# A float32 decoder trunk on one core: the stationary operands' buffers are laid 64 and 32 bytes further apart

## The chip, the core and the metric

The kernel runs on one core of a Trainium2 chip. The metric is the time of one execution on the device, in microseconds (us); of several runs the median is taken. An engine of the core is named as in the profile: PE is TensorE's matmul, PEld TensorE's weight load, DVE VectorE, ACT ScalarE, POOL GpSimd, SP SyncE.

## What is computed

One layer of a "macaron" decoder on 256 tokens of width 2048, in float32. The reference, cut to what matters:

```python
def swiglu(h, w_gate, w_up, w_down):
    return (jax.nn.silu(h @ w_gate) * (h @ w_up)) @ w_down

def hybrid_mixer(h, w_in, conv_w, pool_w, pool_scale, w_out):
    z = h @ w_in                                  # 2048 x 5120
    ...
    return jnp.concatenate([y_attn, y_conv, y_pool], axis=-1) @ w_out

for l in range(DEPTH):                            # DEPTH = 1
    x = x + FFN_RESIDUAL * swiglu(rmsnorm(x, ffn1_norm[l]), ffn1_w_gate[l], ffn1_w_up[l], ffn1_w_down[l])
    x = x + hybrid_mixer(rmsnorm(x, mix_norm[l]), w_in[l], conv_w[l], pool_w[l], pool_scale[l], w_out[l])
    x = x + FFN_RESIDUAL * swiglu(rmsnorm(x, ffn2_norm[l]), ffn2_w_gate[l], ffn2_w_up[l], ffn2_w_down[l])
return rmsnorm(x, final_norm)
```

The feed-forward width is 5632. Between the mixer's two products stand dilated attention, a short convolution and a pooling over windows, all small beside the products.

## The kernel before

Every large product `x @ W` is one job of `gemm` (L138): it makes a block of 256 tokens by 512 columns in PSUM, over row blocks `k` of 128. Both operands are split into a high and a low part, and three matmuls per `k` and token tile `t` are summed (L161 to L163): high activations by high weights, low by high, high by low. In each of them the stationary operand (loaded into the array ahead of the matmul, one weight load per matmul) is a 128x128 piece of the activations, and the moving operand is a 128x512 piece of the weights:

```python
nc.tensor.matmul(acc_of[t][:, t, :], lhsT=hi[:, ts], rhs=wh[:, i, :], start=first, stop=False)
nc.tensor.matmul(acc_of[t][:, t, :], lhsT=lo[:, ts], rhs=wh[:, i, :], start=False, stop=False)
nc.tensor.matmul(acc_of[t][:, t, :], lhsT=hi[:, ts], rhs=wl[:, i, :], start=False, stop=last)
```

The weights come in by SP's queue as `wt` (L171), four row blocks at a time; ACT rounds them into `wh` (L177) and DVE makes `wl`, the rest (L178).

The jobs are named by their sums. `ag` and `au` (gate and up product, 11 column blocks each, in groups of six and five) and `az` (the mixer's input product, 10 column blocks) take the activations `xh`, `xl`: the residual stream, transposed and split by `gained` (L242), four column blocks of `[P, 4, S]`, each 4096 bytes on a partition. `ad` (the down product) takes `hh`, `hl`, the transposed hidden blocks (L255 on, in `ffn`), and `ao` (the mixer's output product) takes `yh`, `yl`; these come from `act_tile` (L44), twelve buffers of 4096 bytes that the mixer's other tiles (`zq`, `qt` and so on) and the last norm's gains `gf` use too. A feed-forward runs 12 jobs `ag`, `au`, then 4 jobs `ad` over 24 row blocks, then 10 jobs and 4 jobs `ad` over 20 row blocks. With 6 matmuls per row block these are 1152, 576, 960 and 480 matmuls; `az` has 960, `ao` 384. Over the kernel `ag`, `au` and `az` have 5184 matmuls, `ad` and `ao` 2496, together 7680.

The order of the instructions is made by a scheduler ahead of the run; the buffers of one tag lie one behind the other in SBUF in the order in which the tags first appear.

Of the kernel before, what the change touches and what calls it, by code (L numbers as in the profile page):

```python
# [9 lines left out]
F32R = mybir.dt.float32r  # L10
# [4 lines left out]
AX = mybir.AxisListType  # L15

P = 128
NB = 512          # columns of one product (one PSUM bank)
CH = 4            # 128-row blocks of a weight per load
EPS = 1e-6  # L20
NEG = -1e30

# [2 lines left out]
def hybrid_trunk(ctx, tc, x, ffn1_norm, ffn1_w_gate, ffn1_w_up, ffn1_w_down, mix_norm, w_in,  # L25
                 conv_w, pool_w, pool_scale, w_out, ffn2_norm, ffn2_w_gate, ffn2_w_up,
                 ffn2_w_down, final_norm, out):
    """Every large product x @ W runs as three one-pass float32r products. An operand a is split
    exactly into ah (a rounded to 12 significant bits) and al = a - ah (at most 12 bits), and
    ah bh + ah bl + al bh is summed in float32."""  # L30
    nc = tc.nc
    B, S, D = x.shape
    T = S // P                      # token tiles
    DN = D // NB                    # column blocks of the model dimension
    FF = ffn1_w_gate.shape[2]
    FB = FF // NB
    KD = D // P
# [3 lines left out]
    pool = ctx.enter_context(tc.tile_pool(name="sb", bufs=1))  # L41
    psum = ctx.enter_context(tc.tile_pool(name="ps", bufs=2, space=bass.MemoryType.PSUM))

    def act_tile(shape, dt, name):  # L44
        return pool.tile(shape, dt, name=name, tag="act", bufs=12)

    def work(shape, name, dt=F32):
        return pool.tile(shape, dt, name=name, tag="wk", bufs=5)
# [1 line left out]
    def tp_tile(name):  # L50
        return psum.tile([P, 2 * NB], F32, name=name, tag="tp", bufs=2)

# [1 line left out]
    xr = [pool.tile([P, T, NB], F32, name=f"x{n}") for n in range(DN)]  # L54
    xv = x[0].rearrange("(t p) d -> p t d", p=P)

    def load_x(n):
        nc.sync.dma_start(out=xr[n], in_=xv[:, :, n * NB:(n + 1) * NB])

    # Per-channel parameters: rows of 128 channels, transposed onto partitions.  # L60
    small, col = [], {}
    for l in range(DEPTH):
        for key, src in (("ffn1", ffn1_norm[l:l + 1]), ("mix", mix_norm[l:l + 1]),
# [26 lines left out]
    make_identity(nc, ident)  # L90
    mhalf = pool.tile([P, T], F32, name="mhalf")
    nc.gpsimd.memset(mhalf, -0.5)
    # While the first loads are under way: ScalarE's tables, TensorE's clock.
    early = pool.tile([P, T], F32, name="early")
    nc.scalar.activation(out=early, in_=mhalf, func=AF.Silu)
    spin = tp_tile("spin")
# [1 line left out]
        nc.tensor.transpose(spin[:, :P], ident, ident)  # L98
    place_params(first_params)

    # C[q, k]: in how many of the patterns key k is for query q; columns 0..127: queries 0..127
    # and keys 0..127; the rest: queries 128..255 and keys 0..255.
    NK = 3 * P
    cnt = pool.tile([P, NK], F32, name="cnt")
    bia = pool.tile([P, NK], F32, name="bia")
# [26 lines left out]
                                    op0=ALU.min)  # L132
        nc.vector.reciprocal(out=rcnt, in_=rcnt)

# [1 line left out]
    high = [None]                   # the last of the weights' roundings  # L136
    later = []                      # work to be put between the products of a job

    def gemm(lhs, w, n0, ks, name, cuts=None, before=None, by_tile=None):
        """lhs: k -> (high, low) [P, S] of block k; w: [K, N] in DRAM, row blocks ks, columns  # L140
        n0.. -> [P tokens, T, NB] in PSUM. cuts: row blocks per load; before(k): called ahead of
        block k's load; by_tile(t, acc): token tile t is multiplied whole before the next one,
        and this is called when it is done."""
        def bank_pair():
            return psum.tile([P, T, NB], F32, name=name, tag="acc", bufs=2)

        acc = bank_pair()
        acc_of = [acc] * T
        if by_tile:
            acc_of = [acc] + [bank_pair() for _ in range(T - 1)]  # L150
        nk = len(ks)
        c0 = 0
        held = []

        def products(t, c0, kk, wh, wl):
            ts = slice(t * P, (t + 1) * P)
            for i, k in enumerate(kk):
                hi, lo = lhs(k)
                first, last = c0 + i == 0, c0 + i == nk - 1
                acc = acc_of[t]  # L160
# [4 lines that stand above are left out]
        cuts = cuts or [CH] * (nk // CH)  # L165
        for ci, m in enumerate(cuts):
            kk = ks[c0:c0 + m]
            if before:
                before(kk[0])
            wt = pool.tile([P, CH, NB], F32, name="wt", tag="wt", bufs=4)  # L170
            nc.sync.dma_start(  # L171
                out=wt[:, :m],
                in_=w[kk[0] * P:(kk[-1] + 1) * P, n0:n0 + NB].rearrange("(k p) n -> p k n", p=P))
            wh = pool.tile([P, CH, NB], F32R, name="wh", tag="wh", bufs=3)
            wl = pool.tile([P, CH, NB], F32R, name="wl", tag="wl", bufs=3)
            with nullcontext() if before else tc.high_priority():
                high[0] = nc.scalar.activation(out=wh[:, :m], in_=wt[:, :m], func=AF.Copy)  # L177
                nc.vector.tensor_sub(out=wl[:, :m], in0=wt[:, :m], in1=wh[:, :m].bitcast(F32))  # L178
            if by_tile and ci >= len(cuts) - 3:
                held.append((c0, kk, wh, wl))  # L180
            else:
                for i, k in enumerate(kk):
                    for t in range(T):
                        products(t, c0 + i, [k], wh[:, i:i + 1], wl[:, i:i + 1])
            c0 += m
            step()
        if by_tile:
            for t in range(T):
                for h in held:
                    products(t, *h)  # L190
                by_tile(t, acc_of[t])
        return acc
# [6 lines left out]
        while later:  # L199
            step()  # L200

# [1 line left out]
    def new_stats():  # L203
        return pool.tile([P, T, DN], F32, name="ss", tag="ss", bufs=2)

# [14 lines left out]
        return rs  # L220

    def transposed(src):
        """[P tokens, T, 4 P] -> PSUM [P, 4, S]"""
        tp = tp_tile("tp").rearrange("p (k s) -> p k s", k=4)
        for i in range(4):
            for t in range(T):
                nc.tensor.transpose(tp[:, i, t * P:(t + 1) * P], src[:, t, i * P:(i + 1) * P], ident)
        return tp
# [1 line left out]
    Q = 32  # L230

    def turned(src, dst):
        """The same by VectorE, SBUF [P, 4, S]: 32 x 32 blocks, moved between the quadrants."""
        sv = src.rearrange("p t (k j c) -> p k t j c", j=P // Q, c=Q)
        dv = dst.rearrange("p k (t a r) -> p k t a r", t=T, a=P // Q)
        for a in range(P // Q):
            for j in range(P // Q):
                nc.vector.transpose(out=dv[j * Q:(j + 1) * Q, :, :, a, :],  # L238
                                    in_=sv[a * Q:(a + 1) * Q, :, :, j, :])
        return dst  # L240

    def gained(n, c0, at_once=False):  # L242
        """Column block n of the residual, times the norm's gain, transposed and split."""
        tp = transposed(xr[n]) if at_once else turned(xr[n], work([P, 4, S], "xt"))
        hi = pool.tile([P, 4, S], F32R, name="xh", tag="xh", bufs=4)
        lo = pool.tile([P, 4, S], F32R, name="xl", tag="xl", bufs=4)
        for i in range(4):
            g = prm[:, c0 + 4 * n + i:c0 + 4 * n + i + 1]
            nc.scalar.activation(out=hi[:, i, :], in_=tp[:, i, :], func=AF.Copy, scale=g)  # L249
# [19 lines left out]
            nc.vector.scalar_tensor_tensor(out=xr[n][:, t, :], in0=acc[:, t, :], scalar=factor,  # L269
                                           in1=xr[n][:, t, :], op0=ALU.mult, op1=ALU.add)  # L270

# [1 line left out]
    def ffn(xt, rs, wg, wu, wd, after, cuts=None, before=None, last_tile=None):  # L273
        """x += 1/2 SwiGLU; after(n) when column block n of x is done; rs() gives the rows' norm
        factors. cuts, before: for the first product; last_tile(t): in place of after() for the
        last column block."""
        ht = {}

        def hidden(j, **first):
# [27 lines left out]
        for j0 in range(0, FB, 6):  # L307
# [3 lines left out]
            ks = range(4 * js[0], 4 * js[-1] + 4)  # L311
# [10 lines left out]
                if done:  # L322
                    after(n)

# [1 line left out]
    def mixer(l, xt, rs_of, after):  # L326
        HD = 64
        rs = rs_of()
# [21 lines left out]
            later.append(turn)  # L350

        def attend(half, i, zs):
            """Two heads, in three steps."""
            parts = (slice(0, P), slice(P, NK))
            st = {}

# [29 lines left out]
            def turn():  # L386
                p = st["p"]
                pt_ps = tp_tile("ptp").rearrange("p (j c) -> p j c", j=2)
                for j in range(2):
                    for a in range(3):  # L390
                        cs = slice(a * P, (a + 1) * P)
                        nc.tensor.transpose(pt_ps[:, j, cs], p[:, j, cs], ident)
                # keys 0..127 by queries 0..255, then keys 128..255 by queries 128..255
                st["pt"] = work([P, 2, NK], "pt")
                nc.scalar.activation(out=st["pt"], in_=pt_ps[:, :, :NK], func=AF.Copy)

# [17 lines left out]
        def attention_half(half):  # L414
# [2 lines left out]
            z_transposed(zs, "k", half)  # L417
            zs["v"] = z_block("v", half)
            pairs = [attend(half, i, zs) for i in range(4)]
            for r in range(6):          # step r - i of pair i  # L420
                def together(r=r):
                    for i in (2, 1, 0, 3):
                        if 0 <= r - i < 3:
                            pairs[i][r - i]()
                later.append(together)
# [76 lines left out]
            residual(acc, n, 1.0)  # L502
            after(n)

# [1 line left out]
    def phase(key, l, body):  # L506
        """Statistics and transposed blocks of the residual for the next sub-layer are made as
        its column blocks are finished."""
        ss, nxt = new_stats(), {}

        def after(n):
# [7 lines left out]
        rs = rstd_of(ss)  # L519
        return nxt, lambda: rs  # L520

    # The first sub-layer's blocks of x are loaded and transposed between its first weights.
    ss0, xt, r0 = new_stats(), {}, []

    def first_block(k):
# [10 lines left out]
            later.extend([lambda: place_params(more), masks, pool_consts])  # L536
        return r0[0]

    # The last norm, by token tiles.
    gf = {}  # L540
    sf = [pool.tile([P, 1, DN], F32, name=f"sf{t}") for t in range(T)]
    xg = {}
# [76 lines left out]
```

## Time and profile before

| | |
|---|---|
| median of 2 runs | 1807.97 us (1807.80 to 1808.13) |
| span of the profiled execution, first to last instruction | 1806.0 us |
| what lies around the span, by the median | 1.97 us |
| PE busy in that span | 1792.2 us (99%) |
| DVE, ACT busy | 1144.4 us (63%), 748.4 us (41%) |
| moved by DMA | 342.32 MB, mean 190 GB/s |

The page names for the profiled execution its span alone; it has no time of its own beside it. A matmul's duration runs from its start to its modelled end and overlaps the next matmul's; how fast PE works is therefore read from the distance between starts, or from a stage's length by its count of matmuls.

### The profile page before, as it was taken

The numbers are of one execution on the slowest core, as the hardware profiler recorded it, in microseconds if no ns is written. First come the engines' busy times: TensorE is split into PE (matmuls) and PEld (weight loads), VectorE is DVE, ScalarE is ACT, GpSimd is POOL, SyncE is SP. The second block draws the span as 40 slices with busy tenths as digits, with TensorE's granted clock in tenths as the row PEclk, the third lists the DMA queues.
The fourth block names the chain that finished last, engine by engine and source line by source line (L and its number), as shares of the span: only waits on it lengthen the run. The fifth ranks groups of instructions, "written<-read, shape, count | busy, mean of one in ns | idle before, by whom it ended". The sixth has DMA issues, their size and how long they took to land.

```text
span 1806.0 us, 19137 instructions
## 1 busy us (share of the span) xinstructions
PE 1792.2 (99%) x7928; PEld 1467.2 (81%) x7928; DVE 1144.4 (63%) x1260; ACT 748.4 (41%) x598; POOL 5.5 (0%) x19
## 2 busy tenths in 40 slices
PE   8999999999999999999999999999999999999998
PEld 7888888888888888887778788888888888888886
DVE  5766666444666677768767796666664446666643
ACT  6434333333344344445444455434433334434332
POOL 0000000000000000000000000000000000000000
PEclk9999999999999999999999999999999999999999
DMA  8656655556566555554545565556655556655652
GB/s 286 210 187 199 197 187 188 192 190 198 188 189 201 193 185 187 190 201 146 187 141 186 172 199 188 187 190 202 194 201 192 187 187 198 197 187 194 219 191 71
DMA packets 172262, 342.32 MB, mean 190 GB/s; under 512 B 5456, under 2 KB 6032, under 8 KB 172176
## 3 DMA queue, kind: packets, MB, share of 16 engines
q1 hardware_dynamic: 171232, 339.76, 57.3%
q10 hardware_dynamic: 944, 1.34, 0.2%
q8 instruction: 62, 1.02, 0.2%
q14 instruction: 24, 0.20, 0.0%
HBM read 338.98 MB, written 2.10 MB: 189 GB/s over the span
## 4 chain that ended last, share of the span: by engine, by line
PE 98%; DVE 1%; DMA 0%; ACT 0%; issue 0%; ACTq 0%; POOLq 0%
PE ad L163 9%; PE ad L161 9%; PE ad L162 9%; PE au L161 9%; PE au L162 9%; PE au L163 9%; PE ag L163 9%; PE ag L161 9%; PE ag L162 9%; PE az L161 4%; PE az L163 4%; PE az L162 4%; PE ao L163 1%; PE ao L162 1%; PE ao L161 1%; DVE wl L178 0%
## 5 line engine op out<-in xcount | busy, mean ns | idle before, releaser
L178 DVE TENSOR_TENSOR wl<-wt,wh 128x2048 fp32r<-128x2048 f32 (+1 forms) x322 | 733.0, 2278 | 554.8 <-ACT wh L177 552.8
L177 ACT ACTIVATE wh<-wt 128x2048 fp32r<-128x2048 f32 (+1 forms) x322 | 613.4, 1905 | 883.1 <-PE au L162 281.4
L161 PE MATMUL ad<-wh,hh 128*128 128x512 f32 x704 | 277.8, 395 | 0.0
L162 PE MATMUL ad<-wh,hl 128*128 128x512 f32 x704 | 277.8, 395 | 0.0
L163 PE MATMUL ad<-wl,hh 128*128 128x512 f32 x704 | 277.6, 395 | 0.0
L161 PE MATMUL ag<-wh,xh 128*128 128x512 f32 x704 | 275.1, 391 | 2.3 <-ACT xh L249 2.3
L163 PE MATMUL ag<-wl,xh 128*128 128x512 f32 x704 | 274.7, 390 | 0.2 <-DVE wl L178 0.2
L162 PE MATMUL ag<-wh,xl 128*128 128x512 f32 x704 | 274.7, 390 | 0.0
L161 PE MATMUL au<-wh,xh 128*128 128x512 f32 x704 | 274.0, 389 | 0.0
L163 PE MATMUL au<-wl,xh 128*128 128x512 f32 x704 | 273.9, 389 | 0.0
L162 PE MATMUL au<-wh,xl 128*128 128x512 f32 x704 | 273.9, 389 | 0.0
L162 PEld LDWEIGHTS ad<-wh,hl 128*128 128x128 f32 x704 | 132.7, 188 | 31.0
L163 PEld LDWEIGHTS ad<-wl,hh 128*128 128x128 f32 x704 | 132.7, 188 | 31.0
L161 PEld LDWEIGHTS ad<-wh,hh 128*128 128x128 f32 x704 | 132.7, 188 | 30.9
L161 PEld LDWEIGHTS ag<-wh,xh 128*128 128x128 f32 x704 | 132.7, 189 | 29.9 <-ACT xh L249 2.5
L238 DVE STREAM_TRANSPOSE ht<-h 32x256 f32<-32x256 f32 x352 | 153.4, 436 | 5.7
L163 PEld LDWEIGHTS ag<-wl,xh 128*128 128x128 f32 x704 | 132.6, 188 | 28.1 <-DVE wl L178 0.6
L162 PEld LDWEIGHTS ag<-wh,xl 128*128 128x128 f32 x704 | 132.6, 188 | 27.6 <-DVE xl L250 0.2
L161 PEld LDWEIGHTS au<-wh,xh 128*128 128x128 f32 x704 | 132.2, 188 | 27.5
L163 PEld LDWEIGHTS au<-wl,xh 128*128 128x128 f32 x704 | 132.2, 188 | 27.4
L162 PEld LDWEIGHTS au<-wh,xl 128*128 128x128 f32 x704 | 132.2, 188 | 27.3
L161 PE MATMUL az<-wh,xh 128*128 128x512 f32 x320 | 126.8, 396 | 0.0
(116 smaller groups left out, 1145.7 us busy)
## 6 DMA issues: line engine op xcount, KB each, us to landing
wt<-in_ffn_w_up_dram SPq DMA_DIRECT2D x88, 1024.0 KB, 5.2
wt<-in_ffn_w_down_dram SPq DMA_DIRECT2D x88, 1024.0 KB, 5.1
wt<-in_ffn_w_gate_dram SPq DMA_DIRECT2D x87, 1024.0 KB, 5.2
wt<-in_w_in_dram SPq DMA_DIRECT2D x40, 1024.0 KB, 5.1
wt<-in_w_out_dram SPq DMA_DIRECT2D x16, 1024.0 KB, 5.2
x<-in_x_dram SPq DMA_DIRECT2D x4, 512.0 KB, 10.0
out_dram<-xg SPq DMA_DIRECT2D x8, 256.0 KB, 3.1
gf<-in_final_norm_dram ACTq DMA_DIRECT2D x2, 512.0 KB, 4.5
```

What stands on the lines that cost most here:

```text
L161: nc.tensor.matmul(acc_of[t][:, t, :], lhsT=hi[:, ts], rhs=wh[:, i, :], start=first, stop=False)
L162: nc.tensor.matmul(acc_of[t][:, t, :], lhsT=lo[:, ts], rhs=wh[:, i, :], start=False, stop=False)
L163: nc.tensor.matmul(acc_of[t][:, t, :], lhsT=hi[:, ts], rhs=wl[:, i, :], start=False, stop=last)
L177: high[0] = nc.scalar.activation(out=wh[:, :m], in_=wt[:, :m], func=AF.Copy)
L178: nc.vector.tensor_sub(out=wl[:, :m], in0=wt[:, :m], in1=wh[:, :m].bitcast(F32))
L238: nc.vector.transpose(out=dv[j * Q:(j + 1) * Q, :, :, a, :], in_=sv[a * Q:(a + 1) * Q, :, :, j, :])
```

## The change

A helper, `stepped`, makes a tile that is `pad` float32 elements wider than it needs to be and hands out a view without them. `act_tile` takes it with 16 elements (64 bytes), `xh` and `xl` in `gained` with 8 (32 bytes). The rest of the difference is comments.

```diff
+    def stepped(shape, dt, name, tag, bufs, pad):
+
+        n = 1
+        for d in shape[1:]:
+            n *= d
+        t = pool.tile([P, n + pad], dt, name=name, tag=tag, bufs=bufs)
+        return t[:, :n].rearrange("p (a b) -> p a b", a=shape[1])
+
     def act_tile(shape, dt, name):
-        return pool.tile(shape, dt, name=name, tag="act", bufs=12)
+        return stepped(shape, dt, name, "act", 12, 16)
...
-        hi = pool.tile([P, 4, S], F32R, name="xh", tag="xh", bufs=4)
-        lo = pool.tile([P, 4, S], F32R, name="xl", tag="xl", bufs=4)
+        hi = stepped([P, 4, S], F32R, "xh", "xh", 4, 8)
+        lo = stepped([P, 4, S], F32R, "xl", "xl", 4, 8)
```

On every engine and queue the built program has the same instructions in the same order as before, with the same buffers by number. What differs is where buffers start. From the built program, on a partition, in bytes:

| buffers | starts before | starts after |
|---|---|---|
| `xh` 0 to 3 | 37696, then every 4096 | 37696, then every 4128 |
| `xl` 0 to 3 | 54080, then every 4096 | 54208, then every 4128 |
| `wt`, `wh`, `wl` | `wh` 103232, `wl` 127808, every 8192 | all 256 further |
| work tiles (`ht`, `xt`, `s`, `h`) | from 153536 | all 256 further |
| `act` 0 to 11 (`hh`, `hl`, `yh`, `yl`) | 175296, then every 4096 | 175552, then every 4160 |

The distance of a stationary buffer's start from the moving operand's (`wh` and `wl` are alike in this), taken modulo 256 bytes:

| buffers | before | after |
|---|---|---|
| `xh` 0, 1, 2, 3 | 0 each | 0, 32, 64, 96 |
| `xl` 0, 1, 2, 3 | 0 each | 128, 160, 192, 224 |
| `act` 0, 1, 2, 3 and on | 128 each | 128, 192, 0, 64, and so on in turn |

The pieces within a buffer lie 512 bytes apart, so the distance holds for all of them. A hidden block's high and low part lie in neighbouring buffers of `act` (11 and 0 count as neighbours), so after the change one of the two has distance 0 or 128 and the other 64 or 192.

## Rows read from the trace of the kernel before

**Rows 1.** The page: span, engines, clock by slices, chain by line.

```profile
span 1806.0 us, 19137 instructions
PE 1792.2 (99%) x7928; PEld 1467.2 (81%) x7928; DVE 1144.4 (63%) x1260; ACT 748.4 (41%) x598; POOL 5.5 (0%) x19
...
PEclk9999999999999999999999999999999999999999
...
PE 98%; DVE 1%; DMA 0%; ACT 0%; issue 0%; ACTq 0%; POOLq 0%
```

**Rows 2.** What PE waited for: total us, times, longest.

```profile
PE ag L161 <- ACT xh L249: 2.3, 1, 2.3
PE spin L98 <- POOL ident masks.py:199: 1.4, 1, 1.4
```

**Rows 3.** Stretches: length, busy (count) of PE, PEld, DVE, ACT, POOL, clock, DMA, GB/s.

```profile
8.83:276.38 267.55, 267.39 (x1177) 220.90 (x1178) 172.46 (x180) 118.00 (x100) 1.38 (x4) 0.99 0.64 210
276.38:410.25 133.87, 133.87 (x578) 108.54 (x577) 68.31 (x49) 46.95 (x26) 0.00 (x0) 1.00 0.57 189
410.25:627.90 217.65, 217.65 (x962) 180.24 (x960) 130.71 (x118) 86.25 (x55) 0.00 (x0) 1.00 0.60 193
627.90:739.45 111.55, 111.55 (x482) 90.45 (x480) 84.57 (x105) 48.10 (x46) 0.00 (x0) 1.00 0.57 189
739.45:982.05 242.60, 242.60 (x1154) 194.89 (x1153) 185.72 (x316) 114.87 (x121) 1.42 (x5) 1.00 0.52 172
982.05:1072.69 90.64, 90.39 (x393) 73.05 (x392) 73.35 (x97) 41.46 (x44) 0.00 (x0) 1.00 0.57 191
1333.83:1467.70 133.87, 133.87 (x578) 108.53 (x576) 68.31 (x49) 46.95 (x26) 0.00 (x0) 1.00 0.57 189
1467.70:1685.35 217.65, 217.65 (x961) 180.24 (x960) 130.71 (x118) 86.26 (x55) 0.00 (x0) 1.00 0.60 193
```

**Rows 4.** Groups of PE within 410.25 to 627.90: count, busy us, mean ns, idle.

```profile
L163 PE MATMUL au<-wl,xh 128*128 128x512 f32 x160 | 62.2, 389 | 0.0
L162 PE MATMUL au<-wh,xl 128*128 128x512 f32 x160 | 62.2, 389 | 0.0
```

**Rows 5.** Groups of PE within 276.38 to 410.25.

```profile
L161 PE MATMUL ad<-wh,hh 128*128 128x512 f32 x192 | 75.8, 395 | 0.0
L162 PE MATMUL ad<-wh,hl 128*128 128x512 f32 x192 | 75.8, 395 | 0.0
```

**Rows 6.** PE in order of time, within `ad`: start us, us, instruction.

```profile
276.38 0.40 PE L161 MATMUL ad<-wh,hh 128*128 128x512 f32 x1
276.62 0.40 PE L162 MATMUL ad<-wh,hl 128*128 128x512 f32 x1
276.85 0.39 PE L163 MATMUL ad<-wl,hh 128*128 128x512 f32 x1
...
278.01 0.40 PE L162 MATMUL ad<-wh,hl 128*128 128x512 f32 x1
278.25 0.40 PE L163 MATMUL ad<-wl,hh 128*128 128x512 f32 x1
```

**Rows 7.** PE in order of time, the first ten matmuls of `ag` after `ad`.

```profile
410.25 0.40 PE L161 MATMUL ag<-wh,xh 128*128 128x512 f32 x1
410.48 0.40 PE L162 MATMUL ag<-wh,xl 128*128 128x512 f32 x1
...
412.33 0.39 PE L161 MATMUL ag<-wh,xh 128*128 128x512 f32 x1
```

**Rows 8.** PE and PEld in order of time, around a matmul with no load beside it.

```profile
32.07 0.19 PEld L163 LDWEIGHTS ag<-wl,xh 128*128 128x128 f32 x1
32.29 0.39 PE L163 MATMUL ag<-wl,xh 128*128 128x512 f32 x1
32.61 0.13 PEld L84 LDWEIGHTS pp<-ident,rows 48*128 48x128 f32 x1 [0.35 <-issue]
```

**Rows 9.** Groups of PE within 32.292 to 32.4: the same matmul's duration in ns.

```profile
L163 PE MATMUL ag<-wl,xh 128*128 128x512 f32 x1 | 0.4, 388 | 0.0
```

**Rows 10.** The page's groups that write the moved buffers: busy, mean ns, idle before.

```profile
L257 DVE TENSOR_TENSOR hl<-ht,hh 128x1024 fp32r<-128x1024 f32 x22 | 26.8, 1219 | 0.0
L256 ACT ACTIVATE hh<-ht 128x1024 fp32r<-128x1024 f32 x22 | 23.4, 1065 | 84.1 <-DVE ht L238 84.1
```

## The prediction

> **What bounds the kernel now.** I read the page first, then what PE waited for, then the stages, then single matmuls in order of time. [...] PE waits for almost nothing: its longest wait is 2.3 us, once, and the second longest 1.4 us [rows 2]. So there is no wait to remove, and the time is the number of matmuls by the distance between their starts. Neither VectorE nor ScalarE sets the end: in the stage from 410.25 us they are busy for 130.71 and 86.25 of 217.65 us [rows 3].
>
> The distance is not the same everywhere, and this is what the reader should see. The first `ad` stage has 576 matmuls in 133.87 us, 232.4 ns each; `ag` and `au` after it 960 in 217.65 us, 226.7 ns each; the second `ad` stage 480 in 111.55 us, 232.4 ns. The second feed-forward repeats it: 133.87 us for 576, 217.65 us for 960 [rows 3]. All of these run at the granted clock 1.00, and the instruction is the same: 512 columns of `wh` or `wl` against a 128x128 piece. Only the buffer of the stationary piece differs, `hh`/`hl` against `xh`/`xl`. The durations differ in the same way, 395 ns against 389 ns [rows 4, 5]. `ao`, which takes `yh`/`yl` from the same twelve buffers as `hh`, takes 90.64 us for 384, 236 ns, with some small work of the mixer in it [rows 3]; I count it with `ad`.
>
> In order of time, `ad` does not run evenly: 276.38 to 276.62 is 0.24 us, the next step 0.23 us, and 0.24 us comes again at 278.01 to 278.25, seven matmuls after the first; those seven take 1.63 us, 232.9 ns each at this grain [rows 6]. After the last `ad` stage of the first feed-forward, `ag` does not start at its own pace: its first nine steps take 410.25 to 412.33, 2.08 us or 231 ns each [rows 7], and only then come the steps of 226.7 ns. So the even pace is a state that the stream has to find, and a disturbed stream takes some nine matmuls to find it.
>
> Is 226.7 ns itself lengthened by the load beside it? At 32.29 us a matmul runs with no weight load beside it: the load of 32.07 ended after 0.19 us and the next starts at 32.61, 0.32 us after the matmul's start [rows 8]. It takes 388 ns [rows 9], and the ones in the even stream, each with a load beside it, 389 ns [rows 4]. So in the even stream the load costs next to nothing, and the 6 ns more of `ad` are the part that an address can give or take.
>
> **The change part by part.** It moves no instruction, adds no wait and no transfer; the order on every engine and queue is the same. It moves buffers. Before, every `xh` and `xl` stands at distance 0 from the moving operand (modulo 256 bytes, the tables of the change) and runs at 226.7 ns; every buffer of `act` stands at distance 128 and runs at 232.4 ns. I take this distance as the cause, an inference from two values: the address in the large differs too, but within `ad` the six blocks of one job lie up to 45 kB apart and all its matmuls take 395 ns on the mean [rows 5].
>
> *Term 1, `xh`/`xl`, 5184 matmuls.* Each of the four column blocks is 1296 of them. Of three loads two are of the high part, one of the low part, so a block keeps the even pace only if both distances do; nine undisturbed matmuls are needed to find it [rows 7], and one load in three is of the other kind. Block 0 now has 0 and 128: the second is the distance of `ad`, so I put it at the pace of `ad`: 1296 x 5.7 ns = 7.4 us more. Blocks 1 to 3 (32 and 160, 64 and 192, 96 and 224) stand at distances that no row shows. The bounds by the nearest rows are 226.7 ns, no loss, and 232.4 ns, 3888 x 5.7 = 22.2 us more. I take the middle, 11.1 us, since neither row is nearer.
>
> *Term 2, `ad` and `ao`, 2496 matmuls.* After the change every pair of high and low part has one member at 0 or 128 and the other at 64 or 192. Half of the pairs contain 128 and stay where they are. The other half, 1248 matmuls, hold 0 and an unknown distance: between 226.7 ns, 7.1 us less, and 232.4 ns, nothing. The middle is 3.6 us less.
>
> *Term 3, the other engines.* ScalarE and VectorE write the moved buffers in 1065 and 1219 ns apiece, 22 times each [rows 10], beside matmuls that do not wait for them [rows 2]. If the new starts slowed these by a tenth it would be 22 x 0.23 = 5 us over the whole run, spread over stages with 17 us and more of idle VectorE each [rows 3]; without that cover it would be those 5 us. I take 0. The shift of `wt`, `wh`, `wl` and the work tiles by 256 bytes keeps their distances among themselves: 0.
>
> Sum: 7.4 + 11.1 - 3.6 = 14.9 us, on the span 1806.0 + 14.9 = 1820.9 us. The median lies 1.97 us above the span, so I forecast 1823 us, 0.8% slower. That is within 2%, which is about what a measurement of this kernel can tell from no change.
>
> [...] First the rows: with a load beside it a matmul takes 389 ns or 395 ns, by the buffer that is loaded [rows 4, 5]. [...]
>
> **The rivals.**
>
> *Nothing happens.* Then what sets the pace of `ad` is not the low part of the address: the buffers of `act` lie above 175 kB, those of `xh` below 71 kB, and both stay there. For it: only two distances are seen, and each goes with one region, so the trace cannot part them. Against it: within either region the buffers spread over tens of kB with one pace. Terms 1 and 2 are 0, the time 1808 us.
>
> *`ad` gains and nothing is lost.* The uneven pace would come of high and low part, or successive loads, at one and the same unlucky distance, and any spreading would end it. For it: `ad` is the only stage with something to gain, and the floor of 389 ns is near. Against it: `xh` and `xl` also stand at one distance, with the best pace of all. 2496 x 5.7 = 14.2 us less: 1794 us, faster than before though not by 2%. This is the rival on the other side of my forecast.
>
> *The unknown distances are worse than 128.* In `ad` a step of 0.24 us stands in every seven [rows 6]. If at some of the distances such steps were the rule, all products would pay. At 236 ns, half way from 232.4 to 240, it would be 5184 x 9.3 + 2496 x 3.6 = 57 us: 1865 us. With `ad` and `ao` as they are, slower by over 2% (36.2 us) begins where `ag`, `au` and `az` pass 226.7 + 36.2 / 5.184 = 233.7 ns. For it: 32 bytes from one buffer to the next is a finer step than any now in the kernel. Against it: a mixed stream has also its quiet loads.
>
> [...]
>
> **How the numbers follow.** My forecast (a mixed stream, 1812 to 1842 us) has 0.42; nothing happens 0.20; `ad` gains alone 0.20; worse distances 0.13; a lower floor 0.05. The forecast's upper end is term 1 in full, 7.4 + 22.2 = 29.6 us, with term 2 at 0: 1837.6 us, and some more for `ao`; its lower end is term 1's block 0 alone with term 2's 7.1 us taken off, 1808 us, so near the second case that I cut at 1812. The range has to take in 1794 us and the full loss: 1792 to 1845 us leaves out the last two cases, 0.18. Faster by over 2% (below 1772 us) is the lower floor, 0.05; slower by over 2% (above 1844 us) the worse distances, 0.13; the rest, 0.82, is within.
>
> **What would show it.** The order of the stages and PE's waits should be as before, and the span's change should lie wholly in the stages' lengths by their counts. Right: `ag` and `au` (960 from about 410 us) at 229 to 232 ns in place of 226.7, their durations at 391 to 395 ns; `ad` at 230 to 232 ns, with jobs of different pace in it. Term 1 is wrong if the 960 still take 217.65 us; term 2, if 576 of `ad` take 133.87 us or fall to 130.6 us (576 x 226.7 ns). If both stay, the low part of the address has nothing to do with it. If any stage falls below 226.7 ns, my reading of the floor is wrong. A new wait of PE for `wl` or `hh` of more than a few us would make term 3 wrong.

## The result and the profile after

The changed kernel takes 1830.37 us (median of 2 runs, 1830.22 to 1830.51) against 1807.97 us: a ratio of 1.0124, 95% interval 1.0080 to 1.0167. It is slower by 22.4 us, within the stated range and within 2%, on the side that was forecast, and the interval leaves out no change. The forecast was 1823 us, 7 us too low.

The page of the kernel after, against [rows 1]: the span has grown by 22.4 us, PE's busy time by 23.2 us and PEld's by 2.5 us; VectorE and ScalarE stand within 0.4 us of where they were, and the clock and the chain are the same.

```profile
span 1828.4 us, 19137 instructions
...
PE 1815.4 (99%) x7928; PEld 1469.7 (80%) x7928; DVE 1144.5 (63%) x1260; ACT 748.8 (41%) x598; POOL 5.5 (0%) x19
...
PEclk9999999999999999999999999999999999999999
...
PE 98%; DVE 1%; DMA 0%; ACT 0%; issue 0%; ACTq 0%; POOLq 0%
```

What PE waited for, against [rows 2]; no wait is new:

```profile
PE ag L169 <- ACT xh L257: 1.4, 1, 1.4
PE spin L106 <- POOL ident masks.py:199: 1.4, 1, 1.4
```

The stages, against [rows 3] (start and end, length, then busy time and count of PE, PEld, DVE, ACT, POOL, the clock, DMA):

```profile
8.90:281.99 273.09, 272.84 (x1177) 221.41 (x1178) 172.40 (x180) 117.99 (x100) 1.39 (x4) 1.00 0.61 206
281.99:414.80 132.81, 132.81 (x577) 108.17 (x576) 68.33 (x49) 46.95 (x26) 0.00 (x0) 1.00 0.56 190
414.80:637.14 222.34, 222.34 (x961) 180.83 (x960) 130.72 (x118) 86.29 (x55) 0.00 (x0) 1.00 0.57 189
637.14:747.65 110.51, 110.51 (x482) 90.19 (x480) 84.54 (x105) 48.12 (x46) 0.00 (x0) 1.00 0.57 191
747.65:994.44 246.79, 246.79 (x1153) 195.40 (x1152) 185.87 (x316) 115.07 (x121) 1.42 (x5) 1.00 0.50 170
994.44:1084.90 90.46, 90.14 (x394) 72.90 (x392) 73.33 (x97) 41.48 (x44) 0.00 (x0) 1.00 0.55 188
1084.90:1351.71 266.81, 266.81 (x1153) 216.99 (x1152) 167.18 (x167) 113.40 (x91) 0.86 (x1) 1.00 0.56 189
1351.71:1485.43 133.72, 133.72 (x578) 108.29 (x576) 68.30 (x49) 46.99 (x26) 0.00 (x0) 1.00 0.56 189
1485.43:1707.77 222.34, 222.34 (x961) 180.83 (x960) 130.73 (x118) 86.27 (x55) 0.00 (x0) 1.00 0.57 189
1707.77:1819.11 111.34, 111.34 (x480) 90.05 (x479) 60.03 (x54) 41.50 (x35) 0.55 (x1) 1.00 0.45 155
```

Take the lengths and subtract those of before. The five stages with `xh` and `xl` lose 5.54, 4.69, 4.19, 5.67 and 4.69 us (the seventh was 261.14 us before), 24.8 us in all or 4.8 ns for each of their 5184 matmuls. The stages with the activation tiles give back 1.06, 1.04, 0.18 and 0.15 us, and the last stands still (111.32 us before): 2.4 us in all. The balance is 22.4 us, the whole change of the span. So nothing has to be sought outside PE's pace: `ag` and `au` now take 222.34 / 960 = 231.6 ns a matmul in place of 226.7.

The groups of PE in the stage from 414.80 show it in the durations too, 393 and 394 ns where [rows 4] had 389:

```profile
L170 PE MATMUL au<-wh,xl 128*128 128x512 f32 x160 | 63.1, 394 | 0.0
...
L169 PE MATMUL au<-wh,xh 128*128 128x512 f32 x160 | 63.0, 393 | 0.0
```

Within one job of that stage, the stretches of the four column blocks (24 matmuls each; in order of time, which is that of the built program, the blocks with distances 0 and 128, 96 and 224, 64 and 192, 32 and 160):

```profile
437.04:442.59 5.55, 5.55 (x25) 1.00 0.57 193
442.59:448.18 5.59, 5.59 (x26) 1.00 0.58 186
448.18:453.73 5.55, 5.55 (x25) 1.00 0.55 190
453.73:459.28 5.55, 5.55 (x26) 1.00 0.57 188
```

231 ns for three of them and 233 ns for the second. No block kept the 226.7 ns.

### The profile page after: what moved, and what is told of

It is laid out like the page before. It is cut to its first block, busy times and chain, and to the rows that moved or that the text cites. A ratio compares the mean times of both kernels' runs of the same rounds, so it can differ in the third digit from the quotient of the medians.

```text
span 1828.4 us, 19137 instructions
## 1 busy us (share of the span) xinstructions
PE 1815.4 (99%) x7928; PEld 1469.7 (80%) x7928; DVE 1144.5 (63%) x1260; ACT 748.8 (41%) x598; POOL 5.5 (0%) x19
## 4 chain that ended last, share of the span: by engine, by line
PE 98%; DVE 1%; DMA 0%; ACT 0%; issue 0%; ACTq 0%; POOLq 0%
PE ad L171 9%; PE au L170 9%; PE au L171 9%; PE au L169 9%; PE ad L170 9%; PE ag L170 9%; PE ag L171 9%; PE ad L169 9%; PE ag L169 9%; PE az L169 4%; PE az L171 4%; PE az L170 4%; PE ao L171 1%; PE ao L170 1%; PE ao L169 1%; DVE wl L186 0%
## 5 line engine op out<-in xcount | busy, mean ns | idle before, releaser
L170 PE MATMUL ag<-wh,xl 128*128 128x512 f32 x704 | 278.5, 396 | 0.0
L170 PE MATMUL au<-wh,xl 128*128 128x512 f32 x704 | 277.7, 394 | 0.0
L169 PEld LDWEIGHTS ag<-wh,xh 128*128 128x128 f32 x704 | 132.6, 188 | 32.4 <-ACT xh L257 1.8
```

## The experiments

All start from the kernel before. "Distance" is the start of the stationary operand's buffer less that of the moving operand's, modulo 256 bytes, as in the tables of the change. A gap is a tile of so many bytes that nothing uses; every buffer behind it lies that much further. All runs of before beside these had medians of 1807.84 to 1807.96 us. Where a run has an interval it is for the ratio to before; the others were timed once.

**One half of the change at a time.** `x_steps` steps only `xh` and `xl`, `act_steps` only the activation tiles. In the experiments the helper `stepped` takes the extra width in bytes; with 0 it makes the plain tile. The cut from `x_steps`:

```diff
-        hi = pool.tile([P, 4, S], F32R, name="xh", tag="xh", bufs=4)
-        lo = pool.tile([P, 4, S], F32R, name="xl", tag="xl", bufs=4)
+        hi = stepped([P, 4, S], F32R, "xh", "xh", 4, 32)
+        lo = stepped([P, 4, S], F32R, "xl", "xl", 4, 32)
```

> Only xh and xl are laid 32 bytes further apart; the activation tiles keep their 4096-byte step and all stand at distance 128 (modulo 256) from the moving operand. Theory (the distance of the stationary buffer from the moving one sets the pace of a matmul): ag and au fall from 226.7 to about 231.6 ns as in the changed kernel, ad stays at 232.4 ns, so the time is 24 to 25 us above the kernel before, some 2 us above the changed kernel. Rival (the step between successive buffers of act costs, or something else that the 256 bytes more move): below 10 us of loss.

> Only the activation tiles are laid 64 bytes further apart; xh and xl stay at distance 0. Theory: ag and au keep 226.7 ns, ad goes from 232.4 to 230 to 232 ns, the time is 1 to 3 us below the kernel before. Rival (the new steps of act cost the time): 10 us or more above it.

`x_steps` took 1832.63 us, 1.0137 (1.0122 to 1.0153); `act_steps` 1805.25 us, 0.9986 (0.9976 to 0.9995). Each half does in its own stages what it does in the whole change, to 0.02 us (`ad`, then `ag` and `au` of `x_steps`):

```profile
281.67:415.54 133.87, 133.87 (x578) 108.53 (x577) 68.32 (x49) 46.95 (x26) 0.00 (x0) 1.00 0.56 189
415.54:637.87 222.33, 222.33 (x961) 180.81 (x960) 130.71 (x118) 86.27 (x55) 0.00 (x0) 1.00 0.57 189
```

The same two stages of `act_steps`:

```profile
275.48:408.29 132.81, 132.81 (x577) 108.28 (x576) 68.33 (x49) 46.96 (x26) 0.00 (x0) 1.00 0.57 190
408.29:625.92 217.63, 217.63 (x962) 180.28 (x961) 130.72 (x118) 86.25 (x55) 0.00 (x0) 1.00 0.57 193
```

So the loss is the 32 bytes alone, 24.8 us, and the 64 bytes bring 2.6 us.

**Distance or region.** `act_0` puts a gap of 128 bytes ahead of the activation tiles, which brings all twelve to distance 0 without steps. `all_64` does that too and moves everything from `xh` on by 64 bytes more. (In these two a memset on POOL writes the gap.)

```diff
     def act_tile(shape, dt, name):
-        return pool.tile(shape, dt, name=name, tag="act", bufs=12)
+        gap("gap_act", 128)
+        return stepped(shape, dt, name, "act", 12, 0)
```

> A gap of 128 bytes ahead of the activation tiles, no steps: all twelve stand at distance 0 from the moving operand, like xh and xl. Theory (the distance, modulo 256): ad and ao fall from 232.4 to 226.7 ns, 2496 x 5.7 = 14.2 us below the kernel before, near 1794 us. Rival (the region, above 175 kB): ad stays at 232.4 ns and the time at 1808 us.

> As the run with the gap of 128 bytes ahead of the activation tiles, and everything from xh on lies another 64 bytes further, so that the moving operand starts at 128 modulo 256 in place of 64, with all distances 0. Theory (only the distance counts): the same as that run, 226.7 ns everywhere, near 1794 us. [...]

`act_0` took 1793.74 us, 0.9922 (0.9907 to 0.9937): 14.1 us below before, where 14.2 were expected. Its first `ad` stage, then `ag` and `au`, are 130.56 / 576 and 217.60 / 960, both 226.7 ns:

```profile
275.54:406.10 130.56, 130.56 (x577) 108.15 (x576) 68.32 (x49) 46.97 (x26) 0.00 (x0) 1.00 0.58 193
406.10:623.70 217.60, 217.60 (x961) 180.27 (x960) 130.73 (x118) 86.25 (x55) 0.00 (x0) 1.00 0.58 193
```

The tiles stayed above 175 kB, so the region is out: 128 bytes moved `ad` by 5.7 ns a matmul. `all_64` took 1797.62 us, 0.9944 (0.9929 to 0.9959). Its later stages have the same lengths; what it lost stands ahead of them, where the first product starts at 10.84 us in place of some 8.8 and its stage takes 268.94 us:

```profile
10.84:279.78 268.94, 266.84 (x1177) 219.86 (x1178) 171.90 (x179) 117.39 (x99) 1.38 (x4) 1.00 0.60 205
279.78:410.34 130.56, 130.56 (x577) 108.20 (x576) 68.32 (x49) 46.97 (x26) 0.00 (x0) 1.00 0.57 194
410.34:627.94 217.60, 217.60 (x961) 180.31 (x960) 130.73 (x118) 86.25 (x55) 0.00 (x0) 1.00 0.58 193
```

So the expectation of the same time missed by 4 us, in the first stage and before it. The trace has a reason there that is not PE's pace: ScalarE rounds a second piece of the weights (at 8.29 us) ahead of the first `xh` (10.31), where before has `xh` first (8.30) and rounds that piece behind it (8.68), and PE's waits for `xh` and `xl` come to 5.6 us in place of 2.3. The moving operand's own start, 128 modulo 256 here and 64 before, makes no difference to the pace, and the floor of 226.7 ns did not move.

**Is it the steps, or the distances?** Four kernels without steps, with gaps between `xl` and the weights' buffers and ahead of the activation tiles, so that all loads of a stage have one distance; in `lo_128` a gap of 128 bytes between `xh` and `xl` makes the low part alone differ. The cut from `x32_act64`:

```diff
+            gap("gap_w", 224)
             wt = pool.tile([P, CH, NB], F32, name="wt", tag="wt", bufs=4)
...
-        return pool.tile(shape, dt, name=name, tag="act", bufs=12)
+        gap("gap_act", 192)
+        return stepped(shape, dt, name, "act", 12, 0)
```

> No steps: all of xh and xl stand at distance 32 from the moving operand, all activation tiles at 64. Theory A (each distance has a pace of its own, and high and low part need not be alike): ag and au at 230 to 233 ns, as the changed kernel has it where 32 is among the distances, ad near 231 to 232 ns; 15 to 40 us above the kernel before. Theory B (any distance is good as long as all loads of a stage have the same): 226.7 ns for ag, au and az, and the time at 1808 us or below.

> No steps: all of xh and xl at distance 96, all activation tiles at 160. Theory A: ag and au near 232 to 233 ns, some 30 us above the kernel before; theory B: 226.7 ns for ag and au, 1808 us or below.

> No steps: all of xh and xl at distance 192, all activation tiles at 224. Theory A: ag and au at 230 to 233 ns, 15 to 35 us above the kernel before; theory B: 226.7 ns for ag and au, 1808 us or below.

> No steps: all of xh at distance 0, all of xl at 128, all activation tiles at 0. If one load in three at 128 keeps the whole stream from its even pace, ag, au and az run at 231.3 ns as the first column block of the changed kernel does, 5184 x 4.6 = 24 us above the run with act at 0, near 1818 us. Rival (each load costs by its own distance alone): two thirds of the matmuls at 226.7 ns and one third at 232.4 ns, 228.6 ns on the mean, near 1804 us.

One time each: 1843.75, 1847.92 and 1820.89 us. `lo_128` took 1816.05 us, 1.0045 (1.0029 to 1.0062). The stages `ad` and then `ag` and `au`, of `x32_act64`:

```profile
283.97:418.37 134.40, 134.40 (x578) 108.29 (x576) 68.33 (x49) 46.99 (x26) 0.00 (x0) 1.00 0.57 188
418.37:642.37 224.00, 224.00 (x962) 180.33 (x961) 130.70 (x118) 86.22 (x55) 0.00 (x0) 1.00 0.58 188
```

of `x96_act160`:

```profile
284.44:418.83 134.39, 134.39 (x577) 108.11 (x576) 68.32 (x49) 46.92 (x26) 0.00 (x0) 1.00 0.57 188
418.83:643.75 224.92, 224.92 (x962) 180.81 (x961) 130.69 (x118) 86.29 (x55) 0.00 (x0) 1.00 0.58 187
```

of `x192_act224`:

```profile
278.67:413.06 134.39, 134.39 (x577) 107.96 (x576) 68.33 (x49) 46.99 (x26) 0.00 (x0) 1.00 0.58 188
413.06:632.81 219.75, 219.75 (x962) 180.29 (x961) 130.72 (x118) 86.23 (x55) 0.00 (x0) 1.00 0.59 191
```

of `lo_128`:

```profile
281.26:411.82 130.56, 130.56 (x577) 108.11 (x576) 68.33 (x49) 46.97 (x26) 0.00 (x0) 1.00 0.58 193
411.82:633.69 221.87, 221.87 (x961) 181.52 (x960) 130.71 (x118) 86.39 (x55) 0.00 (x0) 1.00 0.59 190
```

With the two distances of before this makes a table of the pace, all loads of a stage alike (the stages of the second feed-forward have the same paces in each of these runs, to 0.1 ns):

| distance | 0 | 32 | 64 | 96 | 128 | 160 | 192 | 224 |
|---|---|---|---|---|---|---|---|---|
| ns per matmul | 226.7 | 233.3 | 233.3 | 234.3 | 232.4 | 233.3 | 228.9 | 233.3 |

That high and low part, and one buffer and the next, stand alike does not help: theory B falls. A distance has its own pace, and 0 is the best of the eight. Details of the expectation were off, 32, 64 and 96 slower and 192 faster than I had put them; `x192_act224` was 13 us above before, where 15 to 35 had been expected. `lo_128` shows that a mixed stream is not the mean of its parts: 231.1 ns, where two thirds at 226.7 and one third at 232.4 would be 228.6. One load in three at distance 128 costs 4.4 of the 5.7 ns that all three cost. In the groups of PE in its stage from 411.82 the durations of two of the three matmuls grow, and the third keeps 389 ns:

```profile
L175 PE MATMUL au<-wh,xl 128*128 128x512 f32 x160 | 63.5, 397 | 0.0
...
L174 PE MATMUL au<-wh,xh 128*128 128x512 f32 x160 | 63.4, 396 | 0.0
...
L176 PE MATMUL au<-wl,xh 128*128 128x512 f32 x160 | 62.2, 389 | 0.0
```

**How far does it repeat, and how near must it be?** `x256_act256` has a gap of 256 bytes between `xl` and the weights' buffers and the 128 bytes ahead of the activation tiles. In `x240_act16` the weights' parts, `wh` and `wl` alike, are placed 16 bytes into wider buffers, and a gap of 160 bytes stands ahead of the activation tiles. The line for `wh`:

```diff
-            wh = pool.tile([P, CH, NB], F32R, name="wh", tag="wh", bufs=3)
+            wh = pool.tile([P, CH * NB + 64], F32R, name="wh", tag="wh", bufs=3)[:, 4:4 + CH * NB].rearrange("p (a b) -> p a b", a=CH)
```

> No steps: a gap of 256 bytes between xl and the moving operand and one of 128 bytes ahead of the activation tiles, so that every stationary buffer is at distance 0 modulo 256, but xh and xl no longer at 0 modulo 512. If distances count modulo 256 only: 226.7 ns in ag, au, az and ad, the time as with the 128-byte gap alone, 1794 us. Rival (they count modulo 512 or more): ag, au and az at 229 to 234 ns, 12 us or more above 1794 us.

> No steps: the moving operand's parts are placed 16 bytes into their buffers, so that xh and xl stand at distance 240 and all activation tiles at 16. If the even pace is found only near distance 0 and 16 bytes are near enough: 226.7 to 228 ns in ag, au and ad, 1794 to 1802 us. Rival (it needs the distance 0 itself, or one that is a multiple of 64): 230 to 234 ns in both, 1820 us or more.

`x256_act256` took 1793.93 us, 0.9923 (0.9910 to 0.9937), with 130.56 us in the first `ad` stage and this in `ag` and `au`: 256 bytes more change nothing.

```profile
406.85:624.45 217.60, 217.60 (x961) 180.18 (x960) 130.71 (x118) 86.27 (x55) 0.00 (x0) 1.00 0.60 193
```

`x240_act16` took 1831.53 us. Its `ag` and `au` at distance 240 run at 222.41 / 960 = 231.7 ns. Its `ad` stages at distance 16 do something that neither expectation had (the first, `ag` and `au`, the second, the third, the last):

```profile
281.56:417.87 136.31, 136.31 (x578) 109.78 (x576) 68.33 (x49) 46.88 (x26) 0.00 (x0) 1.00 0.56 186
417.87:640.28 222.41, 222.41 (x962) 180.55 (x960) 130.69 (x118) 86.27 (x55) 0.00 (x0) 1.00 0.59 189
640.28:753.87 113.59, 113.59 (x482) 91.49 (x481) 84.56 (x105) 48.09 (x46) 0.00 (x0) 1.00 0.56 185
1358.60:1489.16 130.56, 130.56 (x577) 108.11 (x576) 68.31 (x49) 47.03 (x26) 0.00 (x0) 1.00 0.58 193
1711.56:1820.13 108.57, 108.57 (x480) 89.91 (x479) 60.04 (x54) 41.54 (x35) 0.55 (x1) 1.00 0.47 158
```

The first two run at 236.6 ns, the slowest pace of the study, the other two at 226.7 ns, the fastest (the last window ends with the start of its last matmul, so it holds 479 steps): the same instructions, the same twelve buffers, the same clock. The first ten steps take 2.36 us in the first stage (from 281.56) and 2.27 us in the third (from 1358.60), and the whole stages have the same means, 136.31 and 130.56 us for 576 matmuls: each keeps the pace of its start.

`ao` stands at distance 16 too, and it has a third pace. Its four jobs read the same buffers of `yh` and `yl`. A stretch of 144 matmuls in the first two runs at 236.7 ns, the slow pace of `ad`, and one of 168 in the last two at 233.3 ns; between them a weight load waited once for `wl`:

```profile
1010.67:1044.75 34.08, 34.08 (x145) 1.00 0.46 153
...
1047.29 0.19 PEld L176 LDWEIGHTS ao<-wl,yh 128*128 128x128 f32 x1 [0.45 <-DVE wl L192]
...
1050.66:1089.86 39.20, 39.20 (x170) 1.00 0.64 210
```

So at this distance the buffers alone do not set the pace. That the wait made the change is not shown. Nor does this run part the distances 16 and 240 from the moving operand's own start, which is 80 modulo 256 here and in no other kernel of the study. The kernel was run once more, to see whether this is chance:

> The kernel with distances 240 and 16 once more, unchanged. In its first profile the two ad stages of the first feed-forward took 236.6 ns a matmul and the two of the second 226.7 ns, from the same buffers. If the state in which a stage enters is settled by the program's own order and lengths, the same two stages are slow again and all times lie within 1 us of 1831.5. If it is chance, another set of ad stages is slow, and the times differ by steps of 576 x 10 = 5.7 us or 480 x 10 = 4.8 us.

1831.58 us (1831.29 to 1831.64 in 4 runs), 1.0130 (1.0114 to 1.0147), and the same stages slow and fast, `ao` with its two paces included (the first and the third `ad` stage):

```profile
281.66:417.97 136.31, 136.31 (x578) 109.72 (x577) 68.33 (x49) 46.88 (x26) 0.00 (x0) 1.00 0.58 185
1358.70:1489.26 130.56, 130.56 (x578) 108.11 (x577) 68.32 (x49) 47.02 (x26) 0.00 (x0) 1.00 0.58 193
```

So which of its paces a stage takes is settled by the program and not by chance: another set of slow `ad` stages would have moved a time by about 5 us, and the four times lie within 0.4 us.

## Why the prediction was right, point by point

*What bounds the kernel.* Right: all of the 22.4 us are in the pace of the 7680 matmuls, none in a wait.

*The cause: the distance modulo 256.* It was inferred from two values that could as well have been two regions. `act_0` (one region, another distance, 14.1 us less) and `x256_act256` (256 bytes more, nothing) bear it out. That it is a matter of the difference and not of the stationary buffer's own start is shown by `x192_act224`, whose `xh` and `xl` stand where they stood before while the weights' buffers have moved; that it is not the moving buffer's own start, by `all_64`. Beyond 256 bytes only the one step of 256 was tried. Nor is the distance the whole of it: at 16 the same distance has three paces.

*Term 1, `xh` and `xl`.* Right in sign and in the rule that both distances must be good, too small in size: 18.5 us were put down, 24.8 measured. For block 0 the rule that one load in three spoils the stream gave 7.4 us; at 5.55 us for 24 matmuls, 231.3 ns, it is 1296 x 4.6 = 6.0 us. `lo_128` shows the rule by itself; that the stream loses because it never has nine undisturbed matmuls, as the prediction had it, is not shown. The step that failed is the middle of the bounds for blocks 1 to 3, 11.1 us. They cost the rest, about 19 us, close to the upper bound of 22.2. The rule had already said that both distances of a block must be good, and with that the upper end was the nearer one; I applied it to block 0 and then split the difference for the others. Nor was 232.4 ns, the nearest row, a bound: streams of one distance run at 233.3 or 234.3 ns at 32, 64, 96, 160 and 224. The sum stayed under 22.2 us because the mixed streams run faster than these, three of the four blocks at 231.3 ns.

*Term 2, the activation tiles.* 3.6 us less were put down, 2.4 us measured in the changed kernel, 2.6 us by `act_steps` alone. That the sizes are near is luck, for the working does not hold: the pairs with 128 did not stay at 232.4 ns, and those with 0 did not all fall below it. Three stretches, placed by the built program: high part at 128 and low at 64 in the first `ad` stage (24 matmuls, 230.0 ns); in the third, 128 and 192 (48 matmuls, 233.3 ns), and 64 and 0 (24 matmuls, 232.9 ns).

```profile
304.14:309.66 5.52, 5.52 (x26) 1.00 0.53 189
...
1396.24:1407.44 11.20, 11.20 (x50) 1.00 0.55 186
...
1412.98:1418.57 5.59, 5.59 (x25) 1.00 0.54 186
```

Stretch by stretch, the first feed-forward runs at 229.2 to 231.1 ns and the second at 230.5 to 234.3 ns, so the gain of 2.1 us is in the first, and in the second gains and losses all but cancel. No pair found the even pace of 226.7 ns. (In the second feed-forward a pair's two buffers are not always neighbours, but one still stands at 0 or 128 and the other at 64 or 192.)

*Term 3, the other engines.* Right: the conversions of `hh` and `hl` took 1062 and 1218 ns after the change, 1065 and 1219 before [rows 10].

```profile
L265 DVE TENSOR_TENSOR hl<-ht,hh 128x1024 fp32r<-128x1024 f32 x22 | 26.8, 1218 | 0.0
...
L264 ACT ACTIVATE hh<-ht 128x1024 fp32r<-128x1024 f32 x22 | 23.4, 1062 | 82.2 <-DVE ht L246 82.2
```

*The floor.* The reading of one matmul with no load beside it, 388 against 389 ns [rows 8, 9], held: no stage of any run went below 226.7 ns a matmul, at any of the ten distances tried. The case of a lower floor, 0.05 in the forecast, has no term that a run shows: the fastest kernel, `act_0`, took 1793.74 us, and that case began below 1772 us.

*The rivals.* That nothing happens fell with the result. That `ad` gains and nothing is lost needed the equal distances to be the harm; `x32_act64` has them and is slower. But its number, 1794 us, is what the distance 0 gives: the gain was there to be had, by one gap of 128 bytes. Distances worse than 128 exist (32, 64, 160 and 224 at 233.3 ns, 96 at 234.3, and the slow stages at 16), but `ag` and `au` of this change, at 231.6 ns, do not reach the 233.7 ns from which the loss passes 2%; `x96_act160`, with such distances in all stages, took 1847.92 us in its one run, 2.2% above before.

At distance 0 the weight load takes next to nothing from the running matmul: 389 ns with a load beside it [rows 4], 388 without [rows 9]. At other distances the pace is slower than there by up to 10 ns a matmul (236.7 against 226.7 ns, `ao` of `x240_act16` at 16).

What stays open is the mechanism below this: why a distance has a pace, why 0 is good, and what decides between the three paces of a stream at distance 16. The two even paces seen most, 226.7 and 233.3 ns, lie 6.7 ns apart; no run here says why.

## What to carry to other kernels

Where TensorE is busy for 99% with float32 products of 512 columns, read the pace from a stage's length by its count of matmuls and compare stages that issue the same instruction: a difference of 2.5% between them was an address, worth 14 us for a gap of 128 bytes. Bring the stationary operands' buffers to the same start, modulo 256 bytes, as the moving operand's, all of them, and do not spread them: one load in three at distance 128 cost 4.4 of the 5.7 ns that all three cost. Measured here is this one shape and type alone. Read the pace in more than one stage, for at one distance it was not the same in all. A run of one uniform setting tells more than a step that mixes eight.

## What the runs showed that was not expected

At distance 16 a stream has three paces, 226.7, 233.3 and 236.7 ns. An `ad` stage keeps for over 100 us the one that it took at its start; `ao` changed once, behind a wait of 0.45 us and with the same buffers. All of it was the same in both profiles. And a stream in which all loads stand alike can be slower than one that mixes the same distances: 233.3 ns at 32 and at 160, but 231.3 ns for the column block of the changed kernel that has the two together.
